# Pooled difference in its running sum's place, pooling output split from PSUM, another order of weight splits and s4 products

## The chip, the cores and the metric

The kernel runs on one core of a Trainium2 chip. The metric is the device time of one execution in microseconds (us), lower is better; it is given as the median of several executions. The engines are TensorE (PE, matrix products), VectorE (DVE), ScalarE (ACT) and GpSimd (POOL); SyncE (SP) only issues transfers. Each runs its own instructions in order and waits on semaphores for the others.

## The reference

One layer of an encoder block on 1024 tokens of width 1024, in float32. One projection gives q, k, v (eight attention heads of 64) and u (512 channels for pooling). Attention looks at a window of 8 x 16 on a token grid of width 64. The pooling takes a centred mean over 2, 4, 8 or 16 tokens, one window size for each group of 128 channels, subtracts the token and maps the difference with a 128 x 128 matrix and a scale per channel:

```
def multiscale_pool(u, w_pool, pool_scale):
    ...
        mean = (cg[:, hi] - cg[:, lo]) / (hi - lo).astype(jnp.float32)[:, None]
        outs.append(mean - uf[:, :, sl])
    d = jnp.stack(outs, axis=2).astype(u.dtype)
    y = jnp.einsum('btgc,gcd->btgd', d, w_pool).reshape(B, T, C)
    return y * pool_scale
...
        a = neighbourhood_attention(q, k, v, rpb[l])
        p = multiscale_pool(u, w_pool[l], pool_scale[l])
        x = x + jnp.concatenate([a, p], axis=-1) @ w_out[l]
        h2 = rms_norm(x, norm2_g[l])
        x = x + (jax.nn.silu(h2 @ w_gate[l]) * (h2 @ w_up[l])) @ w_down[l]
```

## The kernel before, in words

Float32 precision is had from three products: `split` (L118) writes a rounded high part `h` of an operand on ScalarE (L119) and the rest `l` = operand - `h` on VectorE (L120), and `mm3` (L132) multiplies high by high, high by low and low by high into the same PSUM bank. All matmuls have line L85, all transposes on TensorE L90, and all splits L119 and L120, so tiles are told apart by name, the high part of `dh`, `yh`, `w` or `bt_h` among them.

The stages in time: the first pass of projections (to about 40 us), the pooling stage (40 to 110), attention with the other projections between its steps (110 to 250), the output projection W_out with the last attention blocks between its steps (to 366), the gate and up products (366 to 791) and the down products (791 to 1001).

*Pooling.* `u_pool` runs over the four channel groups g. `u_mm(g)` multiplies out `u` of a group in two banks `pu`, which VectorE scales into `u` (L400). `u_win(g)` sums windows by doubling on VectorE (tiles `pw`, L418), corrects the edges (L422, L427), writes the difference `d` (L436), splits it into `dh` and `dl`, and multiplies by the group's matrix into two banks `py`. ScalarE scales these into `y` (L449) and with a permutation back to the order of the tokens; `y` is split once more, and GpSimd's queue stores both parts in `yd`. In the program `u_win(g - 1)` follows `u_mm(g)`; the order on VectorE, ScalarE and the queues is set by a scheduler, that on TensorE from L906 on by the program (`pin`). Weights of the next pass (`w1h`, `w1l` from `raw_w`) are split in between.

*Projections and attention.* `dense` is a generator of projection steps; each step is one run of 3 matmuls `pj` of 128x384. `run(R0)` takes 22 of them, then comes `u_win(3)`, then the space of the pooling's tiles is closed, and the attention's pool `ap` with the bias tiles `nb` is opened in it. `load_bias` (L590) loads two bias tiles on SP's queue, and GpSimd negates them (L591). Scores `s` get their bias on VectorE (L621), ScalarE takes the exponential (L631), GpSimd scales the result `e` (L639), TensorE transposes it (`pt`), it is split, and `po` = p times v follows. `vnh` and `vnl` are the two parts of v. The norm of q and k takes small steps on ScalarE and VectorE (`rsqrt`, L96 to L100) and a product (`qn`, L291), whose result TensorE transposes (`qkt`). `FIRST`, `CYC` and, for the last blocks, `WCYC` tell how many steps `more` takes from `dense` between two attention steps; in the W_out stage a step is 3 matmuls `pw`.

*Gate and up products.* They are formed in a Strassen-Winograd way: seven products of half blocks in place of eight, with weights `11`, `12`, `s1` to `s4`, `22` (`cook_w` splits one of them, L1060) and activations `11`, `21`, `t1` to `t4`, `22` (`split_op`). The first four products (EARLY) go together, part by part: `first` and `second` write bank `x`, `part_y` with `s2` and `t2` writes `y`, `part_z` and `part_w` write `z` and `w`, `part_4` adds `22` by `t4` to `z`, `part_5` adds `s4` by `22` to `w`. Each is 12 matmuls of 512 columns. `norm2` scales the normalized input (L1016), `sub` forms differences (L1030), `settle` ends an output (L1095 adds, L1100 and L1104).

Of the kernel before, what the change touches and what calls it, by code (L numbers as in the profile page):

```python
# [49 lines left out]
def hybrid_block(ctx, tc, xT, xt, w1, wu, rpbx, wpool, wout, wgu, wd, sm, out):  # L50
# [306 lines left out]
    def u_pool(up, hook):  # L357
# [46 lines left out]
        def u_win(g):  # L404
# [38 lines left out]
            for half in range(2):
                ps = bank((stp, pop)[half], f"py_{g}_{half}")
                hs = slice(half * 512, half * 512 + 512)
                mm3(ps, wph, wpl, dh[:, hs], dl[:, hs], True, True)
                pv = ps.rearrange("p (r k c e) -> p r k c e", r=2, k=4, c=8)
                for i in range(2):
                    nc.scalar.activation(  # L449
                        yv[:, 2 * half + i], pv[:, i], AF.Copy, scale=psc_sb[:, g : g + 1]  # L450
                    )
            ys = [slot(F32R, f"y{nm}_{g}") for nm in "hl"]
            split(*ys, y)
# [1154 lines left out]
```

## Time and profile before

| | us |
|---|---|
| median of 3 runs | 1006.23 (1005.81 to 1006.53) |
| the profiled execution | 1007.08 |
| its span | 1005.0 |
| TensorE busy | 989.8 (98%) |
| VectorE busy | 681.9 (68%) |
| ScalarE busy | 416.6 (41%) |
| GpSimd busy | 377.9 (38%) |
| mean granted clock of TensorE | 0.996 of full speed |

The profile is that of one execution; its rows give a start, a duration, the engine, the line, the operation, the tiles written and read and a count, and in brackets the idle time in front of the instruction and what ended it. Matmuls overlap: the duration of one is longer than the distance to the next, and the distance is what it costs. [...]

### The profile page before, as it was taken

To read this page: it belongs to the slowest core of one execution; us is meant where nothing else is said; L and a number is where in the kernel's file an instruction comes from. 1 tells how busy PE (TensorE), PEld (TensorE's weight loads), DVE (VectorE), ACT (ScalarE), POOL (GpSimd) and SP (SyncE) were. 2 spreads that over 40 slices of the span, in tenths; PEclk is the share of its full clock that TensorE was granted. 3 is DMA by queue.
4 is the path that set the end of the run, shared out by engine and by line. 5 is a ranking of instruction groups with operands and counts; after the bars stand their busy time and mean duration, and the time that the engine had idled before them with its cause. 6 is when DMAs were issued, how large, how long until landed. Compare 5 with 4: busy or idle time off the path is not lost.

```text
span 1005.0 us, 13257 instructions
## 1 busy us (share of the span) xinstructions
PE 989.8 (98%) x4801; PEld 843.2 (84%) x4801; DVE 681.9 (68%) x1087; ACT 416.6 (41%) x801; POOL 377.9 (38%) x423
## 2 busy tenths in 40 slices
PE   9997999999999999999999999999999999999998
PEld 9986999999788887878788888888888888888887
DVE  5677676656853789977975554555552599888872
ACT  6633566656643354434233233233242255442500
POOL 0100343323431510079866846846833400000170
PEclk9998999999999999999999999999999999999999
DMA  9411824135922420213423313313317983373302
GB/s 355 185 58 43 267 66 130 55 115 198 340 91 101 151 84 1 71 64 135 159 95 136 127 57 118 137 55 112 135 50 240 361 279 121 108 250 104 126 32 95
DMA packets 56322, 135.89 MB, mean 135 GB/s; under 512 B 5888, under 2 KB 14848, under 8 KB 56256
## 3 DMA queue, kind: packets, MB, share of 16 engines
q1 hardware_dynamic: 48176, 106.45, 31.5%
q0 software_dynamic: 6784, 24.38, 6.5%
q10 hardware_dynamic: 1296, 4.21, 1.1%
q8 instruction: 38, 0.62, 0.2%
q14 instruction: 28, 0.23, 0.1%
HBM read 98.05 MB, written 32.77 MB: 130 GB/s over the span
## 4 chain that ended last, share of the span: by engine, by line
PE 80%; DVE 10%; POOL 5%; issue 2%; ACT 2%; DMA 1%; DVEq 0%; POOLq 0%; ACTq 0%
PE pj L85 12%; PE w L85 9%; PE z L85 9%; PE x L85 8%; PE pw L85 6%; PE pc L85 6%; PE pa L85 6%; PE pd L85 6%; PE pu L85 4%; PE y L85 4%; PE pb L85 3%; PE po L85 3%; PE s L85 2%; PE pt L90 2%; POOL gr L1165 1%
## 5 line engine op out<-in xcount | busy, mean ns | idle before, releaser
L85 PE MATMUL x<-b_h,w 128*128 128x512 f32 x352 | 115.0, 389 | 0.0
L85 PE MATMUL pw<-mx,wo 128*128 128x512 f32 x384 | 90.4, 392 | 0.0
L85 PE MATMUL pj<-w1h,xh 128*128 128x384 f32 x256 | 88.0, 348 | 0.8 <-DVE vnl L306 0.6
L639 POOL TENSOR_SCALAR e<-e,r 64x128 f32<-64x128 f32 (+2 forms) x96 | 53.8, 575 | 90.2 <-DVE r L634 45.8
L85 PE MATMUL pj<-w1l,xh 128*128 128x384 f32 x256 | 85.2, 337 | 0.0
L85 PE MATMUL pj<-w1h,xl 128*128 128x384 f32 x256 | 84.5, 339 | 0.0
L85 PEld LDWEIGHTS pw<-mx,wo 128*128 128x128 f32 x384 | 71.1, 188 | 14.5 <-DVE mx L791 0.4
L1533 POOL TENSOR_TENSOR x2r<-x2r,u 128x512 f32<-128x512 f32 x12 | 23.8, 2015 | 149.8 <-issue 149.8
L1104 POOL TENSOR_TENSOR ur<-ur,gr 128x512 f32<-128x512 f32 x33 | 52.5, 1594 | 72.0 <-DVE ur L1095 49.3
L85 PEld LDWEIGHTS x<-b_h,w 128*128 128x128 f32 x352 | 66.1, 188 | 13.8 <-ACT ur L1109 0.2
L85 PE MATMUL x<-b_l,w 128*128 128x512 f32 x176 | 68.5, 389 | 0.0
L120 DVE TENSOR_TENSOR w_s<-sa,w_s 128x512 fp32r<-128x512 f32 x44 | 53.0, 1207 | 21.9 <-ACT w_s L119 21.5
L119 ACT CAST a_h<-raw_a 128x1024 fp32r<-128x1024 f32 (+1 forms) x42 | 41.0, 979 | 49.3 <-PE pc L85 13.8
L85 PE MATMUL w<-b_h,w_s 128*128 128x512 f32 x176 | 58.1, 391 | 0.6 <-DVE w_s L120 0.6
L85 PE MATMUL y<-bt_h,w_s 128*128 128x512 f32 x176 | 57.6, 390 | 0.8 <-ACT bt_h L119 0.8
L85 PE MATMUL z<-bt_h,w 128*128 128x512 f32 x176 | 57.9, 390 | 0.5 <-DVE gr L1095 0.5
L85 PE MATMUL w<-bt_h,w_s 128*128 128x512 f32 x176 | 57.8, 390 | 0.0
L85 PE MATMUL z<-bt_h,w_s 128*128 128x512 f32 x176 | 57.8, 389 | 0.0
L120 DVE TENSOR_TENSOR a_l<-raw_a,a_h 128x1024 fp32r<-128x1024 f32 (+1 forms) x42 | 49.9, 1193 | 3.4 <-ACT a_h L119 3.1
L85 PEld LDWEIGHTS pj<-w1h,xh 128*128 128x128 f32 x256 | 48.9, 192 | 2.3 <-DVE vnl L306 1.7
L85 PEld LDWEIGHTS pj<-w1h,xl 128*128 128x128 f32 x256 | 48.6, 191 | 0.0
L85 PEld LDWEIGHTS pj<-w1l,xh 128*128 128x128 f32 x256 | 48.5, 190 | 0.1
(275 smaller groups left out, 2639.9 us busy)
## 6 DMA issues: line engine op xcount, KB each, us to landing
raw_a<-gsd SPq DMA_DIRECT2D x77, 256.0 KB, 3.6
raw_g<-in_wgu SPq DMA_DIRECT2D x22, 512.0 KB, 3.9
raw_u<-in_wgu SPq DMA_DIRECT2D x22, 512.0 KB, 4.4
gsd<-gr POOLq DMA_DIRECT2D x22, 512.0 KB, 4.0
raw_d<-in_wd SPq DMA_DIRECT2D x20, 512.0 KB, 4.2
nb<-in_rpbx SPq DMA_DIRECT2D x24, 384.0 KB, 4.8
raw_w<-in_w SPq DMA_DIRECT2D x15, 384.0 KB, 5.3
gsd<-ur POOLq DMA_DIRECT2D x11, 512.0 KB, 3.2
```

The costliest lines, as they stand in the source:

```text
L85: i = nc.tensor.matmul(*a, **k)
L90: i = nc.tensor.transpose(*a)
L119: keep(nc.scalar.copy(h, src))
L120: keepd(nc.vector.tensor_tensor(out=l, in0=src, in1=h.bitcast(F32), op=ALU.subtract))
L639: nc.gpsimd.tensor_scalar(out=out, in0=in0, scalar1=s1, scalar2=1.0, op0=ALU.mult, op1=ALU.mult)
L1104: k(eng.tensor_tensor(out=res[i][c][:, l], in0=src, in1=g, op=ALU.mult))
L1165: tt = lambda **k: keepp(nc.gpsimd.tensor_tensor(**k))
L1533: nc.gpsimd.tensor_tensor(out=q, in0=q, in1=U2[c], op=ALU.add)
```

## The change

The window sums of a group now give way to the difference: `d` is written over the running sum (a view of `cur`), and the slot for `d` is gone. `dh` and `dl` are written in four pieces of 256 columns, permuted to the order of the tokens there, so that the bank `py` holds tokens in order. ScalarE then scales the bank into `yh` at once, and VectorE writes `yl` as the scaled bank minus `yh`, both from PSUM in pieces of 512 columns; the tile `y` and the last split are gone. `u_win(2)` leaves `u_pool` and stands behind the first four steps of `dense` (`R1`). `WCYC` takes one step more at two places. In the first chunk the weight `w_3_11` is loaded and split earlier, into a slot of its own, `w_3_12` and the low part for `s2` later, the second `t2` split stands ahead of an output step, and `part_4(1)` with its weight stands ahead of `part_5(0)`.

```
@@ -34,9 +34,10 @@
 WARM = 17
 CYC = [3, 3, 3, 4, 4, 4, 4, 4, 4, 4, 4, 5, 5, 5, 4, 4]
 R0 = 22
+R1 = 4
 FIRST = [3, 3, 4, 4, 4, 4, 4, 4, 4, 4, 4]
 CYC3 = CYC
-WCYC = [1, 4, 4, 1, 1] + [2] * 6 + [3]
+WCYC = [1, 5, 5, 1, 1] + [2] * 6 + [3]
 POOL_W = [2, 4, 8, 16]
 DGROUPS = [3, 4, 4]
 NPF = NFC // 2
@@ -430,27 +431,28 @@
                     in1=edge[:, g, 9 : 8 + hw],
                     op=ALU.mult,
                 )
-            d = slot(F32, f"d_{g}")
+            d = cur[:, o : o + T]
             dh = slot(F32R, f"dh_{g}")
             dl = slot(F32R, f"dl_{g}")
             nc.vector.scalar_tensor_tensor(
                 out=d, in0=cur[:, o : o + T], scalar=1.0 / w, in1=u[:, o : o + T], op0=ALU.mult, op1=ALU.subtract
             )
-            split(dh, dl, d)
-            y = slot(F32, f"y_{g}")
-            yv = y.rearrange("p (r c k e) -> p r k c e", r=4, c=8, k=4)
+            ys = [slot(F32R, f"y{nm}_{g}") for nm in "hl"]
+            dv = d.rearrange("p (r k c e) -> p r k c e", r=4, k=4, c=8)
+            hv, lv = (a.rearrange("p (r c k e) -> p r k c e", r=4, c=8, k=4) for a in (dh, dl))
+            for r in range(4):
+                split(hv[:, r], lv[:, r], dv[:, r])
             wph, wpl = wps[0][:, g], wps[1][:, g]
             for half in range(2):
                 ps = bank((stp, pop)[half], f"py_{g}_{half}")
                 hs = slice(half * 512, half * 512 + 512)
                 mm3(ps, wph, wpl, dh[:, hs], dl[:, hs], True, True)
-                pv = ps.rearrange("p (r k c e) -> p r k c e", r=2, k=4, c=8)
-                for i in range(2):
-                    nc.scalar.activation(
-                        yv[:, 2 * half + i], pv[:, i], AF.Copy, scale=psc_sb[:, g : g + 1]
-                    )
-            ys = [slot(F32R, f"y{nm}_{g}") for nm in "hl"]
-            split(*ys, y)
+                sc = psc_sb[:, g : g + 1]
+                yh, yl = (a[:, hs] for a in ys)
+                nc.scalar.activation(yh, ps, AF.Copy, scale=sc)
+                nc.vector.scalar_tensor_tensor(
+                    out=yl, in0=ps, scalar=sc, in1=yh.bitcast(F32), op0=ALU.mult, op1=ALU.subtract
+                )
             for nm in range(2):
                 nc.gpsimd.dma_start(out=yd[g][nm], in_=ys[nm].bitcast(F32))
 
@@ -464,9 +466,8 @@
             if g == 3:
                 cook_w1(1, 2)
                 cook_w1(1, 3)
-            if g:
+            if g in (1, 2):
                 u_win(g - 1)
-            if g in (1, 2):
                 cook_w1(1, g - 1)
         return u_win
 
@@ -904,7 +905,9 @@
 
     dense = g_dense()
     pin = True
-    run(R0)
+    run(R1)
+    u_win(2)
+    run(R0 - R1)
     u_win(3)
     su.close()
     sa = ExitStack()
@@ -1058,7 +1061,7 @@
         sums[i]["s1"], sums[i]["s2"] = s1, s2
 
     def cook_w(i, o):
-        if i < EARLY and o in ("11", "12"):
+        if i < EARLY and o in ("11", "12") and (i, o) != (3, "11"):
             w = rg.tile([P, 2, 512], F32R, tag="w", name=f"w_{i}_{o}")
         else:
             w = slot(F32R, f"w_{i}_{o}", [P, 2, 512])
@@ -1242,6 +1245,8 @@
     r6 = square1(6)
     hl.append(tok_split(r6, "s6"))
     w_full(7, 1)
+    fetch_w(3)
+    cook_w(3, "11")
     r7 = square1(7)
     hl.append(tok_split(r7, "s7"))
     cook_w(2, "11")
@@ -1255,11 +1260,8 @@
     tok_sum(1, hl[2], False, True)
     scale2(1, (lambda: sum_w(2, nc.vector, keepd),))
     first(1, xs[1], range(2, 4))
-    fetch_w(3)
     act_op("t2")
     norm2(1, 0, 2)
-    cook_w(3, "11")
-    cook_w(3, "12")
     second(0, xs[0])
     settle(0, 0, 0, xs[0])
     second(1, xs[1])
@@ -1269,14 +1271,15 @@
     norm2(1, 1, 3)
     first(2, xs[2])
     split_op("t2", 0, t2[0])
-    cook_w(0, "s2")
     first(3, xs[3])
+    cook_w(3, "12")
     second(2, xs[2])
     second(3, xs[3])
     sub(x2[1], x2[5], x2[1])
     sub(t2[1], x2[7], x2[1])
+    cook_w(0, "s2")
+    split_op("t2", 1, t2[1])
     settle(1, 0, 0, xs[1])
-    split_op("t2", 1, t2[1])
     cook_w(1, "s2")
     cook_w(2, "s2")
     settle(2, 0, 0, xs[2])
@@ -1318,18 +1321,18 @@
     cook_w(0, "22")
     part_w(2, mmp)
     part_z(3, mmp)
+    cook_w(1, "22")
     act_op("22")
     for q in range(2):
         split_op("22", q, x2[6 + q])
     cook_w(0, "s4")
     part_w(3, pop)
-    cook_w(1, "22")
     part_4(0)
+    part_4(1)
     cook_w(1, "s4")
     part_5(0)
     fetch_w(4)
     cook_w(2, "22")
-    part_4(1)
     cook_w(2, "s4")
     part_5(1)
     fetch_w(5)
```

On TensorE, at the end of the pooling's `u` products, stood before (`pu_1` is the second half of the last group, `py_0` and `py_1` the halves of group 2, `pj_0` the first projection bank; the last number of a name is a count of tiles):

```order
L85 MATMUL pu_1_948<-xl_212,wuh_820 128x512
L85 MATMUL pu_1_948<-xh_211,wul_821 128x512
L85 MATMUL py_0_998<-dh_992,wp_hl 128x512
L85 MATMUL py_1_1004<-dh_992,wp_hl 128x512
L85 MATMUL py_0_998<-dl_993,wp_hl 128x512
L85 MATMUL py_0_998<-dh_992,wp_hl 128x512
L85 MATMUL py_1_1004<-dl_993,wp_hl 128x512
L85 MATMUL py_1_1004<-dh_992,wp_hl 128x512
L85 MATMUL pj_0_1028<-w1h_0_814,xh_164 128x384
```

and stands now:

```order
L86 MATMUL pu_1_952<-xh_211,wul_823 128x512
L86 MATMUL pj_0_999<-w1h_0_816,xh_164 128x384
...
L86 MATMUL pj_1_1000<-w1h_0_816,xl_174 128x384
L86 MATMUL py_0_1034<-dh_1021,wp_hl 128x512
L86 MATMUL py_0_1034<-dl_1022,wp_hl 128x512
L86 MATMUL py_0_1034<-dh_1021,wp_hl 128x512
L86 MATMUL py_1_1040<-dh_1021,wp_hl 128x512
```

The six `py` of group 2 have moved behind twelve `pj`, and the two halves follow one another in place of alternating.

On VectorE, the rows from the edge corrections of group 2's window sum (`pw_4_987`, now `pw_4_1017`) to its low part `dl`; before:

```order
L422 TENSOR_TENSOR pw_4_987<-pw_4_987,edge 128x4
L427 TENSOR_TENSOR pw_4_987<-pw_4_987,edge 128x3
L400 TENSOR_TENSOR u_918<-pu_0_921,rstd_bc 128x8x4x8 x2
L120 TENSOR_TENSOR yl_907<-y_893,yh_906 128x1024
L120 TENSOR_TENSOR w1l_1_913<-raw_w_1_1_714,w1h_1_912 128x768
L120 TENSOR_TENSOR w1l_2_976<-raw_w_1_2_818,w1h_2_975 128x768
L400 TENSOR_TENSOR u_918<-pu_1_948,rstd_bc 128x8x4x8 x2
L418 TENSOR_TENSOR pw_1_1125<-u_918 128x1055
L120 TENSOR_TENSOR w1l_3_980<-raw_w_1_3_916,w1h_3_979 128x768
L436 SCALAR_TENSOR_TENSOR d_991<-pw_4_987,u_824 128x1024
L418 TENSOR_TENSOR pw_2_1127<-pw_1_1125 128x1052
L120 TENSOR_TENSOR dl_993<-d_991,dh_992 128x1024
```

and now:

```order
L453 SCALAR_TENSOR_TENSOR yl_893<-py_0_902,sm_sb,yh_892 128x512
L453 SCALAR_TENSOR_TENSOR yl_893<-py_1_908,sm_sb,yh_892 128x512
L423 TENSOR_TENSOR pw_4_1017<-pw_4_1017,edge 128x4
L428 TENSOR_TENSOR pw_4_1017<-pw_4_1017,edge 128x3
L121 TENSOR_TENSOR w1l_1_917<-raw_w_1_1_714,w1h_1_916 128x768
L121 TENSOR_TENSOR w1l_2_980<-raw_w_1_2_820,w1h_2_979 128x768
L437 SCALAR_TENSOR_TENSOR pw_4_1017<-pw_4_1017,u_826 128x1024
L401 TENSOR_TENSOR u_922<-pu_0_925,rstd_bc 128x8x4x8 x2
L121 TENSOR_TENSOR w1l_3_984<-raw_w_1_3_920,w1h_3_983 128x768
L121 TENSOR_TENSOR dl_1022<-pw_4_1017,dh_1021 128x4x8x8 x4
```

The difference (L436, now L437) stood behind both evacuations of `pu` and the first sum of group 3 (`pw_1_1125`), and now stands ahead of them.

On TensorE at the last attention block, around the transposes `pt_3` of the probabilities, to the first `po_3`; before:

```order
L90 MATMUL pt_3_1_3837<-ident,e_3_1_1_3707 128x128
L90 MATMUL pt_3_2_3838<-ident,e_3_1_1_3707 128x128
L85 MATMUL pw_0_0_3823<-mx_1_0_3132,wo_0_0_3086 128x512
L85 MATMUL pw_0_0_3823<-mx_1_1_3133,wo_0_0_3086 128x512
L85 MATMUL pw_0_0_3823<-mx_1_0_3132,wo_0_1_3087 128x512
L85 MATMUL pw_0_0_3823<-mx_1_0_3132,wo_0_0_3086 128x512
L85 MATMUL pw_0_0_3823<-mx_1_1_3133,wo_0_0_3086 128x512
L85 MATMUL pw_0_0_3823<-mx_1_0_3132,wo_0_1_3087 128x512
L85 MATMUL po_3_3861<-pt_h,vnh_2380 128x2x128
```

and now:

```order
L86 MATMUL pw_0_0_3831<-mx_1_0_3140,wo_0_1_3095 128x512
L91 MATMUL pt_3_0_3850<-ident,e_3_0_0_3704 128x128 x3
...
L91 MATMUL pt_3_1_3851<-ident,e_3_0_1_3708 128x128 x3
L91 MATMUL pt_3_1_3851<-ident,e_3_1_1_3721 128x128
L91 MATMUL pt_3_2_3852<-ident,e_3_1_1_3721 128x128
L86 MATMUL po_3_3869<-pt_h,vnh_2388 128x2x128
```

The six `pw` that stood between the last `pt` and `po` have moved ahead; the same count has moved ahead of the last `qkt`.

## Rows read from the trace of the kernel before

**Rows 1.** The page's busy line of all engines: us, share of the span, instructions.

```profile
PE 989.8 (98%) x4801; PEld 843.2 (84%) x4801; DVE 681.9 (68%) x1087; ACT 416.6 (41%) x801; POOL 377.9 (38%) x423
```

**Rows 2.** The view of TensorE's waits: who waited for whom, us in total, times, the longest.

```profile
PE py L85 <- ACT dh L119: 5.3, 1, 5.3
PE qkt L90 <- DVE qn L291: 1.2, 1, 1.2
...
PE y L85 <- ACT bt_h L119: 0.8, 1, 0.8
PE y L85 <- DVE bt_l L120: 0.8, 1, 0.8
...
PE w L85 <- DVE w_s L120: 0.6, 1, 0.6
```

**Rows 3.** The timeline of TensorE from 87 to 110 us: start, duration, line, operation, out<-in, shapes, count, and in brackets the idle time in front and its releaser.

```profile
87.77 0.39 PE L85 MATMUL pu<-xl,wuh 128*128 128x512 f32 x1
87.99 0.39 PE L85 MATMUL pu<-xh,wul 128*128 128x512 f32 x1
93.67 1.22 PE L85 MATMUL py<-dh,wp_hl 128*128 128x512 f32 x2 [5.29 <-ACT dh L119]
...
97.21 0.52 PE L85 MATMUL pj<-w1l,xh 128*128 128x384 f32 x1
97.53 0.52 PE L85 MATMUL pj<-w1h,xl 128*128 128x384 f32 x1
...
100.15 0.33 PE L85 MATMUL pj<-w1l,xh 128*128 128x384 f32 x1
100.32 0.33 PE L85 MATMUL pj<-w1h,xl 128*128 128x384 f32 x1
...
109.33 0.39 PE L85 MATMUL py<-dh,wp_hl 128*128 128x512 f32 x1
```

**Rows 4.** The windows of 2 us of TensorE: the window, its length, busy time and count, the granted clock, the share of the transfer engines and GB/s.

```profile
90.00:92.00 2.00, 0.00 (x0) 1.00 0.00 0
...
94.00:96.00 2.00, 1.88 (x4) 0.50 0.00 0
...
98.00:100.00 2.00, 2.00 (x11) 0.74 0.00 0
```

**Rows 5.** The timeline of VectorE from 79 to 93 us.

```profile
79.62 1.25 DVE L418 TENSOR_TENSOR pw<-pw 128x1048 f32<-128x1048 f32 x1
...
82.98 0.76 DVE L400 TENSOR_TENSOR u<-pu,rstd_bc 128x256 f32<-128x256 f32 x2 [1.84 <-PE pu L85]
84.08 1.23 DVE L120 TENSOR_TENSOR yl<-y,yh 128x1024 fp32r<-128x1024 f32 x1 [0.34 <-ACT yh L119]
85.22 1.82 DVE L120 TENSOR_TENSOR w1l<-raw_w,w1h 128x768 fp32r<-128x768 f32 x2
88.42 0.76 DVE L400 TENSOR_TENSOR u<-pu,rstd_bc 128x256 f32<-128x256 f32 x2 [1.38 <-PE pu L85]
...
90.45 0.95 DVE L120 TENSOR_TENSOR w1l<-raw_w,w1h 128x768 fp32r<-128x768 f32 x1
91.32 1.22 DVE L436 SCALAR_TENSOR_TENSOR d<-pw,u 128x1024 f32<-128x1024 f32 x1
```

**Rows 6.** What pieces of each size take: ScalarE's cast of 1024 columns and its four activations of 256 (timeline); VectorE's subtraction of 256 columns (the view of groups by form, 60 to 125 us: count, busy us, mean ns) and its three-operand form of 512 (timeline).

```profile
92.57 1.04 ACT L119 CAST dh<-d 128x1024 fp32r<-128x1024 f32 x1 [6.32 <-DVE d L436]
110.23 1.57 ACT L449 ACTIVATE y<-py,sm_sb 128x256 f32<-128x256 f32 x4 [1.67 <-PE py L85]
```

```profile
L120 DVE TENSOR_TENSOR kl<-qkt,kh 128x256 fp32r<-128x256 f32 x2 | 0.8, 418 | 0.4 <-ACT kh L119 0.4
```

```profile
378.04 2.08 DVE L1016 SCALAR_TENSOR_TENSOR x<-x,sm_sb,y 128x512 f32<-128x512 f32 x3
```

**Rows 7.** The first bias tiles: their load on SP's queue, GpSimd's negation and VectorE's first use (timelines), and the line on landing times of all bias loads from the view of the tile `nb`.

```profile
101.60 1.04 SPq L590 DMA_DIRECT2D nb<-in_rpbx  x2
107.13 1.64 POOL L591 TENSOR_SCALAR nb<-nb 128x768 f32<-128x768 f32 x2 [6.00 <-DVE v L260]
111.76 0.56 DVE L621 CUSTOM_DVE_ANT_0 e<-s,nb 128x384 f32<-128x384 f32 x1 [1.78 <-PE s L85]
```

```profile
DMA to landing us min/median/max: 3.1/4.8/9.0
```

**Rows 8.** The last attention block in the W_out stage: VectorE's and GpSimd's rows at 256 us, then the transposes, the splits of their result and the first product on TensorE, ScalarE and VectorE at 315 to 318 us (timelines).

```profile
256.84 2.40 DVE L99 SCALAR_TENSOR_TENSOR rsq_q<-rsq_q,v 128x8 f32<-128x8 f32 x1
256.81 1.62 POOL L639 TENSOR_SCALAR e<-e,r 64x128 f32<-64x128 f32 x4
...
315.15 1.25 PE L90 MATMUL pt<-ident,e 128*128 128x128 f32 x10
315.78 1.41 ACT L119 CAST pt_h<-pt 128x512 fp32r<-128x512 f32 x3 [3.78 <-PE pt L90]
316.40 1.62 DVE L120 TENSOR_TENSOR pt_l<-pt,pt_h 128x512 fp32r<-128x512 f32 x3 [8.81 <-ACT pt_h L119]
317.63 0.28 PE L85 MATMUL po<-pt_h,vnh 128*128 128x256 f32 x1
```

**Rows 9.** The timeline of VectorE in the first chunk: a row behind an idle stretch, the pair of low parts of `w_3`, and the low part of the first s4 weight.

```profile
371.15 0.69 DVE L120 TENSOR_TENSOR sq_hl_s<-sq,sq_hl_s 128x512 fp32r<-128x512 f32 x1 [1.35 <-ACT sq_hl_s L119]
...
380.69 1.29 DVE L120 TENSOR_TENSOR w<-raw_u,w 128x512 fp32r<-128x512 f32 x2
...
428.09 0.68 DVE L120 TENSOR_TENSOR w_s<-raw_g,w_s 128x512 fp32r<-128x512 f32 x1
```

More of the change, by code (lines that the diff above doesn't have):

```diff
@@ L36 @@
 R0 = 22
+R1 = 4
 FIRST = [3, 3, 4, 4, 4, 4, 4, 4, 4, 4, 4]
 CYC3 = CYC
-WCYC = [1, 4, 4, 1, 1] + [2] * 6 + [3]
+WCYC = [1, 5, 5, 1, 1] + [2] * 6 + [3]
 POOL_W = [2, 4, 8, 16]
@@ L432, in u_win @@
                 )
-            d = slot(F32, f"d_{g}")
+            d = cur[:, o : o + T]
             dh = slot(F32R, f"dh_{g}")
@@ L438, in u_win @@
             )
-            split(dh, dl, d)
-            y = slot(F32, f"y_{g}")
-            yv = y.rearrange("p (r c k e) -> p r k c e", r=4, c=8, k=4)
+            ys = [slot(F32R, f"y{nm}_{g}") for nm in "hl"]
+            dv = d.rearrange("p (r k c e) -> p r k c e", r=4, k=4, c=8)
+            hv, lv = (a.rearrange("p (r c k e) -> p r k c e", r=4, c=8, k=4) for a in (dh, dl))
+            for r in range(4):
+                split(hv[:, r], lv[:, r], dv[:, r])
             wph, wpl = wps[0][:, g], wps[1][:, g]
@@ L446, in u_win @@
                 mm3(ps, wph, wpl, dh[:, hs], dl[:, hs], True, True)
[L447 to L453, printed above, removed]
+                sc = psc_sb[:, g : g + 1]
+                yh, yl = (a[:, hs] for a in ys)
+                nc.scalar.activation(yh, ps, AF.Copy, scale=sc)
+                nc.vector.scalar_tensor_tensor(
+                    out=yl, in0=ps, scalar=sc, in1=yh.bitcast(F32), op0=ALU.mult, op1=ALU.subtract
+                )
             for nm in range(2):
@@ L466, in u_pool @@
                 cook_w1(1, 3)
-            if g:
+            if g in (1, 2):
                 u_win(g - 1)
-            if g in (1, 2):
                 cook_w1(1, g - 1)
@@ L906, in hybrid_block @@
     pin = True
-    run(R0)
+    run(R1)
+    u_win(2)
+    run(R0 - R1)
     u_win(3)
@@ L1060, in cook_w @@
     def cook_w(i, o):
-        if i < EARLY and o in ("11", "12"):
+        if i < EARLY and o in ("11", "12") and (i, o) != (3, "11"):
             w = rg.tile([P, 2, 512], F32R, tag="w", name=f"w_{i}_{o}")
@@ L1244, in hybrid_block @@
     w_full(7, 1)
+    fetch_w(3)
+    cook_w(3, "11")
     r7 = square1(7)
@@ L1271, in hybrid_block @@
     split_op("t2", 0, t2[0])
-    cook_w(0, "s2")
     first(3, xs[3])
+    cook_w(3, "12")
     second(2, xs[2])
@@ L1277, in hybrid_block @@
     sub(t2[1], x2[7], x2[1])
+    cook_w(0, "s2")
+    split_op("t2", 1, t2[1])
     settle(1, 0, 0, xs[1])
-    split_op("t2", 1, t2[1])
     cook_w(1, "s2")
@@ L1320, in hybrid_block @@
     part_z(3, mmp)
+    cook_w(1, "22")
     act_op("22")
@@ L1325, in hybrid_block @@
     part_w(3, pop)
-    cook_w(1, "22")
     part_4(0)
+    part_4(1)
     cook_w(1, "s4")
@@ L1331, in hybrid_block @@
     cook_w(2, "22")
-    part_4(1)
     cook_w(2, "s4")
```

3 lines of the change are left out of this document (removed).

## The prediction

> **What bounds the kernel now.** I read the page's busy line first: TensorE is busy 98% of the span [rows 1], so an edit can win only what TensorE idles, or what it does at a lower clock. The view of TensorE's waits then lists nearly all of that idle time in a handful of single events [rows 2]; one of 5.3 us stands out, the rest are about 1 us or less each. The timeline of TensorE places the large one: the last `pu` matmul starts at 87.99, the next instruction, `py` of pooling group 2, only at 93.67, released by the high cast of `d` on ScalarE [rows 3]. The windows show what follows: the granted clock was 1.00 until the idle stretch, 0.50 in 94 to 96 and 0.74 in 98 to 100 [rows 4], which is the lower level (1.2 GHz) for about 5 us. The matmuls say the same: 128x384 ones start 0.32 us apart at 97.21 and 97.53, 0.17 apart at 100.15 and 100.32 [rows 3].
>
> What that place costs in all: at full clock a 512-wide matmul takes 0.227 us of TensorE (87.77 to 87.99) and a 384-wide one 0.174. Between the end of `pu` (87.99 + 0.23 = 88.22) and `py` of group 3 stand 6 `py` and 66 `pj`: 6 x 0.227 + 66 x 0.174 = 12.85 us. `py` of group 3 could start at 101.07 and starts at 109.33 [rows 3]: 8.2 us lost, of which 5.3 are idle and 2.9 the lower clock.
>
> Why `d` was late stands in VectorE's rows [rows 5]. The windows of group 2 are summed by 80.87 (79.62 + 1.25). Then VectorE's own order puts the evacuation of `pu` of group 3 first, which waits 1.84 us for TensorE, `yl`, two weight splits, the second evacuation (another 1.38 us of waiting), the first sum of group 3 and a third weight split, and only then `d` at 91.32. VectorE was waiting for TensorE, and TensorE then for VectorE.
>
> **The change, part by part.**
>
> *Group 2 moved (R1 = 4).* Twelve `pj` matmuls now stand between the last `pu` and `py` of group 2, so TensorE asks for `dh` at 88.22 + 12 x 0.174 = 90.3. On VectorE `d` now stands ahead of the evacuations of `pu`: after 80.87 come the two new low parts of group 1 (2 x 0.69, the 128x512 form of [rows 6]), the edges (0.2), two weight splits (1.82, [rows 5]), then `d` (1.22): done at about 85.5. `dh` is now four ScalarE pieces of 128x256; the nearest row is four activations of that size, 1.57 us together, against 1.04 for the one 1024-wide cast that they replace [rows 6]: done at 87.1. `dl` is four VectorE pieces of 0.42 [rows 6] = 1.67 where one of 1.22 stood, behind one evacuation (0.76) and one weight split (0.95): done at about 88.9. Both are ready 1.4 us or more before TensorE asks. So the idle stretch goes, and with it the low clock, which only followed it: **-8.2 us**; bounds -8.2 and, if the pieces come 1.5 to 2 us later than I sum them, about -6. The evacuations of `pu` that now wait behind `d` (by some 2.5 us) hold no bank that TensorE needs before about 92.4, the fourth group of `pj`.
>
> [...]
>
> *Output of the pooling split from PSUM.* Per group ScalarE loses four activations (1.57) and a 1024-wide cast (1.04) and gains two 128x512 activations (about 0.6 each, a bound from 0.5 to 0.7 by the 128x256 and 1024-wide rows); VectorE loses a 1.22 us subtraction and gains two of 0.69. With the pieces of `dh` and `dl` added, ScalarE is 0.9 us a group lighter and VectorE 0.6 heavier. Neither bounds this stage once `d` is early; I cost it at nothing. The cover is the 54 `pj` between the two groups; without it the 0.6 would lie open.
>
> *`d` in place of the running sum.* The bias tiles `nb` take the space of the pooling's tiles, so their load has to wait for the last reader. Before, that was the write of `d` of group 3, and the load was issued at 101.60, to land 3.1 to 9.0 us later (median 4.8); GpSimd negated the two tiles from 107.13, and the scores' first VectorE step came at 111.76 [rows 7]. Now the last reader is the last piece of `dl` of group 3, and the load can go out at about 100.7, only 0.9 earlier, while TensorE is 8.2 us earlier. With the median landing the tiles are negated by 107.2, VectorE has the first scores done by about 109, then comes `vnl` of the next projection (0.35), which TensorE's `pj` needs by about 109.5. **+0.4 us**, bounds 0 and +1.2; beyond that it is a rival, below.
>
> *W_out steps (WCYC).* Six `pw` matmuls (6 x 0.227 = 1.36 us) go ahead of the last block's transposes `qkt`. There TensorE waited 1.2 us for `qn` [rows 2], whose chain held a 128x8 operation that took 2.40 us from 256.84 while GpSimd scaled `e` [rows 8]. The six cover that: -1.2, bounds 0 and -1.2. They are taken from between the last `pt` and `po`. There `pt` starts at 315.15 and ends its issue near 316.2, ScalarE casts from 315.78, VectorE subtracts from 316.40 (three, 1.62), and `po` began at 317.63, after the six [rows 8]. Without them TensorE reaches `po` at 316.2 and can't end it before the low parts come, around 317.5: **+1.3**, bounds +0.8 and +1.5. Together +0.1.
>
> *First chunk.* The high product's weight `w_3_11` (one VectorE piece, half of the 1.29 us pair at 380.69) goes into an idle 1.35 us at 371.15 [rows 9], `w_3_12` and `w_0_s2` go back behind the `t2` split. The TensorE waits at `y` for `bt_h` and `bt_l` are 0.8 each [rows 2]; the second half of that input comes about 1.2 us sooner, yet VectorE is busy all through, and the low part of `w_0_s2` then is the next to be late. I take **-0.6**, bounds 0 and -1.6. `fetch_w(3)` goes ahead on SP's queue with its DMAs and delays nothing that TensorE waits for.
>
> *Order of s4.* The wait of 0.6 at `w` is for the low part of the s4 weight, made at 428.09 [rows 2, 9]. Twelve matmuls of `part_4(1)` (12 x 0.227 = 2.7 us) now stand before it, and that weight is delayed only by one more split (0.68). **-0.6**, bounds -0.6 and 0.
>
> Sum: -8.2 + 0.4 + 0.1 - 0.6 - 0.6 = -8.9. The profiled execution took 1007.08 us, so 998.2; it lay 0.85 above the median of the runs (1006.23), so **997.4**.
>
> **The rivals.**
>
> *Late bias tiles (about 1000).* If `nb` lands at 7 rather than 4.8 us, `vnl` comes at about 111.5 and `pj` waits 2 us; again at the next block for 0.5: -8.9 + 2.5 = -6.4, 999.8. For it speaks that SP's load moved by 0.9 us and TensorE by 8.2; against, that the load has the queue for itself [rows 7]. It comes out the same by a second mechanism: GpSimd's two negations (1.64 us, [rows 7]) now fall beside VectorE's small rsqrt steps, and one such step took 2.40 us beside GpSimd's work at 256.84 [rows 8]; 1.6 us more before `vnl`, 999.6. [...]
>
> *The small orders give nothing (about 999.5).* W_out wins nothing at `qkt`, since what GpSimd and VectorE do there merely shifts, and loses 1.3 at `po`; the first chunk stays bound by VectorE: -8.2 + 0.4 + 1.3 - 0.6 = -7.1, 999.1. For it speaks VectorE's unbroken work there; against, that the six matmuls are there whatever VectorE does.
>
> *The gap moves on (about 1001).* `d` comes early, but the pieces of `dl`, written through a permuted view, take twice the 0.42 us, or `dl` waits for a slot that the store of group 1's `y` still reads: `py` of group 2 waits some 2 us, and the clock may fall for a part: -8.9 + 2 + 2 = -4.9, 1001.3.
>
> *Slower (about 1008).* The in-place `d` ties the first bias load to `dl` of group 3. If the load lands 11 us or more after its issue, VectorE's in-order queue holds `vnl` behind the scores' first step until about 115.5, `pj` stands still for 6 us from 109.5, and the clock drops as it did after 88 (another 2.9): the whole gain is given back, and a second block with the same 2 us late makes it 1008. It decides from 11 us on; the longest landing in the trace is 9.0 [rows 7], so it is unlikely.
>
> **How the numbers follow.** Forecast 997.4 (995.5 to 998.5): 0.55. Late bias tiles: 0.18. Small orders nothing: 0.12. The gap moves on: 0.07. Slower: 0.04; and 0.04 for no change that can be told. A measurement of this kernel can tell about 0.2% (2 us) from no change, so faster means below 1004.2. The low end of the range takes the favourable bounds of the small terms (-8.2 - 1.2 + 0.8 - 1.6 - 0.6 = -10.8: 995.4), the high end takes in the first two rivals and most of the third: 995.2 to 1001.5. Faster 0.91, same 0.05, slower 0.04.
>
> **What would show each step.** In the profile after: no wait of `py` on ScalarE and a granted clock of 1.00 from 88 to 100; `py` of group 3 near 101 (right: -8.2). A new wait of `pj` on `vnl` near 109 to 112 of under 1 us (if 2 or more, the first rival). No wait at the last `qkt`; a wait of `po` on `pt_h` or `pt_l` of about 1.3 near 306 (if none, the W_out term is a gain). The waits of `y` on `bt_h` and `bt_l` cut by half, none of `w` on `w_s` after `part_4`. The prediction is wrong if `py` of group 2 still waits or if the clock falls elsewhere in the first 130 us.

## The result and the profile after

The changed kernel takes 997.95 us (median of 4 runs, 997.62 to 998.92) against 1006.38 (1005.81 to 1006.72) for the kernel before beside it: 0.9918 of its time, 95% interval 0.9901 to 0.9936. On another chip, beside the last experiments, it took 999.78 (998.31 to 1000.74) against 1006.10: 0.9933, interval 0.9919 to 0.9947. Two executions of the experiments, one of the first run with 5673 us and one of the seventh with 1228 us, lie far outside all others and stand in no median, range or view below. The profiled execution took 997.62 us with a span of 995.5, 9.5 less than before. The forecast was 997.4, in a range of 995.2 to 1001.5, with 0.55 on 995.5 to 998.5; the median of the second chip lies outside the narrower one.

TensorE's waits after, the view that answers to [rows 2]:

```profile
PE z L86 <- DVE gr L1098: 1.1, 1, 1.1
PE pj L86 <- DVE vnl L307: 0.7, 1, 0.7
PE po L86 <- ACT pt_h L120: 0.6, 1, 0.6
PE w L86 <- DVE bt_l L121: 0.5, 1, 0.5
PE po L86 <- DVE pt_l L121: 0.4, 1, 0.4
PE y L86 <- DVE bt_l L121: 0.3, 1, 0.3
```

The 5.3 us of `py` are gone, as are the waits of `qkt`, of `y` for `bt_h` and of `w` for `w_s`. New are the two of `po` and the one of `w` for `bt_l`, and `z` waits 1.1 where it waited 0.5.

The timeline of TensorE and the windows of its granted clock, as a share of full speed, where [rows 3, 4] had the gap:

```profile
87.91 0.39 PE L86 MATMUL pu<-xh,wul 128*128 128x512 f32 x1
...
90.24 0.39 PE L86 MATMUL py<-dh,wp_hl 128*128 128x512 f32 x1
...
100.99 0.39 PE L86 MATMUL py<-dh,wp_hl 128*128 128x512 f32 x1
```

```profile
90.00:92.00 2.00, 2.00 (x12) 1.00 0.00 0
...
94.00:96.00 2.00, 2.00 (x14) 1.00 0.66 266
```

No idle time, clock 1.00, and `py` of group 3 at 100.99 in place of 109.33. The timelines of VectorE and of ScalarE show why, against [rows 5]: after the low parts of group 1 (80.70 to 82.10) and two weight splits comes `d` (written into `pw`, L437), and only then an evacuation of `pu` (L401).

```profile
82.17 1.82 DVE L121 TENSOR_TENSOR w1l<-raw_w,w1h 128x768 fp32r<-128x768 f32 x2
83.91 1.22 DVE L437 SCALAR_TENSOR_TENSOR pw<-pw,u 128x1024 f32<-128x1024 f32 x1
85.04 0.74 DVE L401 TENSOR_TENSOR u<-pu,rstd_bc 128x256 f32<-128x256 f32 x2
...
86.57 1.42 DVE L121 TENSOR_TENSOR dl<-pw,dh 128x256 fp32r<-128x256 f32 x4
```

```profile
85.21 1.33 ACT L120 CAST dh<-pw 128x256 fp32r<-128x256 f32 x4 [2.61 <-DVE pw L437]
```

`d` ends at 85.13, the four pieces of `dh` at 86.54, those of `dl` at 87.99. The bias tiles, against [rows 7] (timelines of SP's queue, GpSimd and VectorE, and the one wait of `pj` on TensorE):

```profile
99.97 0.80 SPq L591 DMA_DIRECT2D nb<-in_rpbx  x2
103.39 0.83 POOL L592 TENSOR_SCALAR nb<-nb 128x768 f32<-128x768 f32 x1 [8.08 <-DVE yl L453]
104.26 0.56 DVE L622 CUSTOM_DVE_ANT_0 e<-s,nb 128x384 f32<-128x384 f32 x1 [0.21 <-POOL mixf L68]
...
123.15 0.45 PE L86 MATMUL pj<-w1h,xh 128*128 128x384 f32 x1 [0.67 <-DVE vnl L307]
```

The load goes out at 99.97, only 1.6 us earlier than before, but GpSimd can start on the first tile 3.4 us later; TensorE doesn't wait near 109. It waits at 122.5 for `vnl`, 0.67 us, where it waited 0.64 before, 8 us later.

The view of waits doesn't show all that TensorE loses. Its lead, by which a matmul starts earlier than the same one of the kernel before, is 8.34 us at `py` of group 3 and 7.92 at the scores of the next block (120.01 before, 112.09 now). The 0.42 between them are lost in the first scores, which go in pairs; the rows of one pair before and now:

```profile
111.45 0.33 PE L85 MATMUL s<-kh,qh 64*128 64x384 f32 x2
```

```profile
103.11 0.75 PE L86 MATMUL s<-kh,qh 64*128 64x384 f32 x2
```

The second of the pair starts at 103.42, 0.31 behind the first. The first of VectorE's two new `yl` pieces (two from 102.61 on, 1.44 us) had by then just read its bank `py`; that the scores wait for it is named as the releaser only in the profile of the kernel with `d` in its own slot, below.

### The profile page after: what moved, and what is told of

It reads as the page before. It is cut to its first block, busy times and chain, and to the rows that moved or that the text cites. A ratio compares the mean times of both kernels' runs of the same rounds, so it can differ in the third digit from the quotient of the medians.

```text
span 995.5 us, 13274 instructions
## 1 busy us (share of the span) xinstructions
PE 986.9 (99%) x4801; PEld 841.5 (85%) x4801; DVE 685.0 (69%) x1103; ACT 412.4 (41%) x801; POOL 376.0 (38%) x423
## 4 chain that ended last, share of the span: by engine, by line
PE 50%; DVE 0%; issue 0%
PE z L86 9%; PE w L86 8%; PE x L86 8%; PE pc L86 6%; PE pa L86 6%; PE pd L86 6%; PE y L86 4%; PE pb L86 3%; PE pd_end L86 0%; DVE gr L1098 0%; DVE w L121 0%; DVE x2r L1494 0%
```

## The experiments

**The move undone (first and fifth run).** `u_win(2)` goes back to its place, all else stays:

```
-            if g in (1, 2):
+            if g:
                 u_win(g - 1)
+            if g in (1, 2):
                 cook_w1(1, g - 1)
...
-    run(R1)
-    u_win(2)
-    run(R0 - R1)
+    run(R0)
```

> The changed kernel with u_win(2) back in u_pool, so that py of group 2 follows the last pu at once again; the new splits, the in-place d and everything else stay. Theory A (d was late by its place in VectorE's order, and the rewritten u_win alone brings it ahead of the evacuations of pu): VectorE's order is that of the changed kernel, dh is ready near 86.5 and dl near 88.0, TensorE asks at 88.1: idle under 0.5 us, granted clock 1.00, 998 us within 1.5. Theory B (the twelve pj matmuls are the cover): the idle time of about 5 us before py comes back with the low clock, 1004 to 1006 us.

> The kernel of the first experiment once more, since the execution that was profiled there ran five times too long throughout. Theory A (VectorE's order): before py of group 2 under 0.5 us of idle time, d done at about 85.1 and dl at 88.0, granted clock 1.00, 998 to 1001 us. Theory B (the twelve pj): about 5 us idle, low clock, 1004 to 1006.

Measured: 998.85, 999.49 and 1001.12 in the first, 0.9935 of the kernel before (0.9918 to 0.9952); 999.82 (997.40 to 1000.59) in the second, 0.9940 (0.9927 to 0.9953). The timeline of TensorE in the second:

```profile
87.87 0.39 PE L86 MATMUL pu<-xh,wul 128*128 128x512 f32 x1
88.10 0.62 PE L86 MATMUL py<-dh,wp_hl 128*128 128x512 f32 x2
...
100.92 0.39 PE L86 MATMUL py<-dh,wp_hl 128*128 128x512 f32 x1
```

`py` of group 2 follows the last `pu` without a gap, and `py` of group 3 starts at 100.92, as in the changed kernel. Theory A: the twelve `pj` are not what closes the gap, as long as `d` is written in place (more below).

**The move alone.** The kernel before, and nothing but:

```
+R1 = 4
...
-            if g:
+            if g in (1, 2):
                 u_win(g - 1)
-            if g in (1, 2):
                 cook_w1(1, g - 1)
...
-    run(R0)
+    run(R1)
+    u_win(2)
+    run(R0 - R1)
```

> The kernel before with R1 = 4 alone (u_win(2) behind twelve pj); splits, d, y, WCYC and first chunk as before. VectorE's order keeps d behind both evacuations of pu. Theory A: dh still comes at about 93.6, TensorE asks at 90.3 and waits about 3.3 us; the twelve pj (2.1 us) are all that is won if the clock falls as before, 1004 us, or 1001 if it stays at 1.00. Theory B: the move alone brings the whole gain of this place, 998 to 999 us.

Measured: 1004.31 (1003.34 to 1005.18), 0.9983 (0.9974 to 0.9992). VectorE's `d` and TensorE's `py` of group 2 (timelines):

```profile
90.73 1.22 DVE L437 SCALAR_TENSOR_TENSOR d<-pw,u 128x1024 f32<-128x1024 f32 x1
```

```profile
93.14 0.50 PE L86 MATMUL py<-dh,wp_hl 128*128 128x512 f32 x1 [3.24 <-ACT dh L120]
94.43 0.79 PE L86 MATMUL py<-dl,wp_hl 128*128 128x512 f32 x1 [0.80 <-DVE dl L121]
...
106.50 0.39 PE L86 MATMUL py<-dh,wp_hl 128*128 128x512 f32 x1
```

`d` still starts at 90.7, TensorE waits 3.2 and 0.8 us, the clock falls again (0.54 in 94 to 96), and `py` of group 3 comes only 2.8 us earlier, 0.6 of which this execution was ahead before the place (its last `pu` starts at 87.40 against 87.99). Both runs together: the gain comes from the rewritten `u_win`, under which the scheduler puts `d` ahead of the evacuations. The move adds 2 us of cover that this order doesn't need. Which part of the rewriting brings the order about (the pieces, the output from PSUM, `d` in place) was tested for the last alone.

**The idle time filled.** The kernel before, with work that nobody reads in the gap:

```
+            if g == 2:
+                fill = bank(stp, "fill")
+                for _ in range(22):
+                    mm(fill, wph, xh[KC - 1][:, 512:1024], start=True, stop=True)
```

> The kernel before with 22 added matmuls of 512 columns into an unused bank between the last pu and py of group 2; their result is not read. They take 22 x 0.227 = 5.0 of the 5.3 us of idle time, so that only the clock differs. Theory (the 2.9 us behind the idle stretch are the lower clock, and it falls because TensorE stood still): py starts at about 93.7 as before, the granted clock stays 1.00, py of group 3 starts near 106.5 and the time is 2.9 us lower, 1003.5. Rival (the low clock has another cause): 1006.4, clock 0.5 in 94 to 98 as before.

Measured: 1005.26 (1003.21 to 1005.57), 0.9983 (0.9973 to 0.9994). TensorE's timeline, and its windows further on:

```profile
88.22 5.15 PE L85 MATMUL fill<-xh,wp_hl 128*128 128x512 f32 x22
93.68 0.73 PE L85 MATMUL py<-dh,wp_hl 128*128 128x512 f32 x2 [0.31 <-ACT dh L119]
95.03 0.51 PE L85 MATMUL py<-dl,wp_hl 128*128 128x512 f32 x1 [0.61 <-DVE dl L120]
...
107.51 0.39 PE L85 MATMUL py<-dh,wp_hl 128*128 128x512 f32 x1
...
390.23 0.50 PE L85 MATMUL y<-bt_h,w_s 128*128 128x512 f32 x1 [0.79 <-ACT bt_h L119]
391.49 0.50 PE L85 MATMUL y<-bt_l,w_s 128*128 128x512 f32 x1 [0.76 <-DVE bt_l L120]
```

```profile
392.00:394.00 2.00, 2.00 (x7) 0.65 0.00 0
394.00:396.00 2.00, 2.00 (x6) 0.50 0.00 0
```

The clock stays at 1.00 from 84 to 118, so it was the idle time that let it fall. But `py` of group 3 comes only 1.8 us earlier (107.51 against 109.33), not 2.9. `py` starts at the same time as before (93.68 against 93.67; the 0.31 for `dh` are what the filling left of the old gap), and the first `py` with `dl` too (95.03 against 95.02): `dl` is late by itself. At full clock the two `py` ahead of it take 2 x 0.227 of these 1.35 us, so 0.9 us are lost to `dl` even at full clock. The median is only 0.9 us lower: behind the two waits of `y` in the first chunk the clock fell in this profile (0.65, 0.50), which it did not in that of the kernel before (1.00 in both windows, waits of 0.84 and 0.76).

**Later bias tiles.** In `load_bias` of the changed kernel:

```
+            for _ in range(3 if p == b == 0 else 1):
                 keeps(nc.sync.dma_start(out=nb, in_=rpbx[p, COLPAT[b], :, H]))
```

> The changed kernel with the first two bias tiles loaded three times over, each load behind the one before, so that they come about 7 us later (near 110.5 in place of 103.4). First rival's mechanism (the bias tiles are close to the critical path): VectorE's scores wait until about 111.5, TensorE reaches the scores of the next block at 112.1 and waits 1 to 3 us for their banks, 999 to 1001 us; if VectorE's queue also holds vnl, 2 us more. Rival (a late load costs nothing here): 998 us within 0.7.

Measured: 1003.32 (1002.32 to 1004.83), 0.9970 (0.9959 to 0.9982). VectorE's first scores, and the longest of TensorE's waits for them (timelines):

```profile
112.52 0.56 DVE L623 CUSTOM_DVE_ANT_0 e<-s,nb 128x384 f32<-128x384 f32 x1 [4.85 <-POOL nb L593]
```

```profile
115.77 0.92 PE L86 MATMUL s<-kh,qh 64*128 64x384 f32 x2 [1.36 <-DVE m L623]
```

The scores come 8.3 us later, and the kernel takes about 4 us more than the changed one (0.9970 against 0.9918 and 0.9933), more than either theory said: besides waits of 0.5 and 1.4 us for the scores and 1.3 for `vnl` the clock is 0.66 in 115 to 120. The added loads also push back all that stands behind them on SP's queue (the first `vsh` goes out at 109.62 in place of 100.88), so the 4 us aren't the price of the bias tiles alone. GpSimd has the first tile 11.2 us after the load's issue, the delay from which the prediction's rival *Slower* has the whole gain given back: about half of it was. The step that this rival needed, `vnl` held behind the scores, did not come: VectorE has one `vnl` at 106.69, ahead of the scores at 112.52. So late bias tiles cost; in the changed kernel they were not late.

**Old first chunk, old s4, old WCYC.** Three kernels, each the changed one with one order set back. The first, the weights of the first chunk:

```
-        if i < EARLY and o in ("11", "12") and (i, o) != (3, "11"):
+        if i < EARLY and o in ("11", "12"):
...
-    fetch_w(3)
-    cook_w(3, "11")
     r7 = square1(7)
...
+    fetch_w(3)
     act_op("t2")
     norm2(1, 0, 2)
+    cook_w(3, "11")
+    cook_w(3, "12")
...
+    cook_w(0, "s2")
     first(3, xs[3])
-    cook_w(3, "12")
...
-    cook_w(0, "s2")
-    split_op("t2", 1, t2[1])
     settle(1, 0, 0, xs[1])
+    split_op("t2", 1, t2[1])
```

> The changed kernel with the old order of the first chunk's weights (w_3_11, w_3_12, w_0_s2 and the second t2 split; the order of s4 stays new). Theory: the two waits of 0.8 us at y come back in place of 0.32 and 0.45, +0.8 us: 998.8. The clock fell behind that pair of waits in the profiles of two experiments so far, though not in that of the kernel before; where it does, 2 us more, 1000.8, so that the single times lie in two groups. Rival (VectorE is behind by as much either way): 998.0 and no second group.

Measured: 1000.20 (998.76 to 1002.16), 0.9955 (0.9942 to 0.9968). TensorE's two waits come back:

```profile
384.28 0.49 PE L86 MATMUL y<-bt_h,w_s 128*128 128x512 f32 x1 [0.79 <-ACT bt_h L120]
...
385.54 0.50 PE L86 MATMUL y<-bt_l,w_s 128*128 128x512 f32 x1 [0.77 <-DVE bt_l L121]
```

They are 0.79 and 0.77. In the changed kernel one of 0.32 is left there, and the 0.45 stand elsewhere, at `w` (397.21), where this kernel has none. By TensorE's lead the first chunk wins 0.60 in the changed kernel (8.11 ahead of it, 8.71 behind) and 0.03 here (8.01, 8.04): 0.6 is what the order is worth in the profiles. The times can't show it: the median is 1.0 to 1.5 above those of the two kernels below, in times that spread over 3.4. The clock stayed at 1.00 behind the waits in this profile; two of the five executions had a mean clock of 0.998, which is no proof of the place.

The second, the order of s4:

```
-    cook_w(1, "22")
     act_op("22")
...
+    cook_w(1, "22")
     part_4(0)
-    part_4(1)
...
     cook_w(2, "22")
+    part_4(1)
```

> The changed kernel with part_4(1) and the 22 weight of 1 back behind part_5(0). Theory: the wait of 0.6 us of w for the low part of the s4 weight comes back, 998.5. The wait of 1.1 us of z for gr near 490 stays if GpSimd's row of products sets it, or falls to 0.5 if this order made it: 997.9. Rival: the whole of it is given back further on, 998.0 and no wait at w.

Measured: 998.66 (998.13 to 1001.90), 0.9940 (0.9928 to 0.9952), and no profile that tells of waits. Inconclusive; that the wait of `w` goes is seen in the profile after alone, and whether the new order made the longer wait of `z` stays open.

The third, the table of W_out:

```
-WCYC = [1, 5, 5, 1, 1] + [2] * 6 + [3]
+WCYC = [1, 4, 4, 1, 1] + [2] * 6 + [3]
```

> The changed kernel with the old WCYC. Theory (a swap of one wait for another): the wait of 1.2 us of qkt for qn comes back, the two waits of po (0.6 and 0.4) go, 998.2. Rival (the change at qkt is pure gain): 999.1, with the waits of po unchanged. Rival (the change costs): 997.0, with no wait at qkt.

Measured: 999.16 (996.24 to 1000.97), 0.9938 (0.9926 to 0.9951). From the view of TensorE's waits:

```profile
PE pj L86 <- DVE vnl L307: 2.0, 1, 2.0
...
PE qkt L91 <- DVE qn L292: 1.2, 1, 1.2
```

The wait of `qkt` is back, no `po` waits: a swap, as the theory had it. By TensorE's lead from the first `pw` to the last, W_out wins 0.27 in the changed kernel (7.84 to 8.11) and 0.02 here (6.34 to 6.36). Such a difference can't be seen in times that spread over 4 us.

**What spreads them: the changed kernel again, and with fewer loads.** The second is the changed kernel with two lines in `load_bias`:

```
+            if p == 0 and b == 1:
+                nbs[p, 1, H] = nbs[p, 0, H]
+                continue
```

> The changed kernel itself, as the measure for the three kernels beside it on the same chip: 0.992 of the kernel before. Its wait of pj for vnl near 122 us is 0.7 us in its first profile and 1.6 to 2.0 in those of the last experiments, in a stretch in which weight and bias loads land one behind the other; if that is a matter of when they land and not of the edits, it lies in the same range here.

> The changed kernel without the bias load of the second block (it uses the first block's bias tiles, so the bias of that block is another one), 768 KB less between 107 and 122 us. Theory (since TensorE is 8 us earlier there, the loads are what is late at 122): the wait of pj for vnl near 122 falls under 0.4 us, 0.5 to 1.5 us less than the changed kernel, single times closer together. Rival (that wait comes from VectorE's and GpSimd's own work): 0.7 to 2.0 as before, same time.

Measured: 999.78 (998.31 to 1000.74) and 996.92 (996.63 to 997.55), 0.9933 (0.9919 to 0.9947) and 0.9909 (0.9895 to 0.9922). Of the first: TensorE's wait, two windows of its clock, and what ScalarE and GpSimd waited for ahead of it; then TensorE's wait in the second:

```profile
123.35 0.45 PE L86 MATMUL pj<-w1h,xh 128*128 128x384 f32 x1 [1.75 <-DVE vnl L307]
```

```profile
124.00:126.00 2.00, 2.00 (x12) 0.56 0.00 0
126.00:128.00 2.00, 2.00 (x13) 0.58 0.00 0
```

```profile
115.34 0.83 ACT L120 CAST w1h<-raw_w 128x768 fp32r<-128x768 f32 x1 [3.97 <-DMA raw_w<-in_w]
```

```profile
116.38 2.28 POOL L592 TENSOR_SCALAR nb<-nb 128x768 f32<-128x768 f32 x2 [2.45 <-DMA nb<-in_rpbx]
```

```profile
122.11 0.45 PE L86 MATMUL pj<-w1h,xh 128*128 128x384 f32 x1 [0.53 <-DVE vnl L307]
```

With 768 KB less the wait is 0.53 in place of 1.75 (under 0.4 was forecast), the clock stays up, and the times lie within 0.9 us of each other. The edit also takes two negations off GpSimd, so by itself it doesn't tell the loads from GpSimd's work. The rows of the first do: ScalarE stands still until a weight load lands, with its exponentials behind that cast (from 116.08), and GpSimd until bias tiles land, with its scaling of `e` behind them (118.64; 116.87 in the second). So the landing of the loads is the cause of the larger wait.

In the first, TensorE's lead falls from 8.79 to 6.18 us over this stretch, 2.6 in all with about 1.5 of it the clock; in the first profile of the same kernel it falls by 0.1. Of the 2.5 between them 0.9 give back a head start: this execution was already 0.9 further ahead at its last `pu` (87.02 against 87.91), while the loads landed at about the same time. Among its five executions the three with a mean granted clock of 0.998 took 999.78 to 1000.74, the two at 1.00 took 998.31 and 998.53; that this is the clock behind 122 us is seen for the profiled one alone.

**`d` in its own slot.** The changed kernel with

```
-            d = cur[:, o : o + T]
+            d = slot(F32, f"d_{g}")
```

> The changed kernel with d in a slot of its own again; splits, y and the move stay. VectorE's order has d of group 2 behind the first evacuation of pu, and dl in two halves around the second. Theory (in place or not matters little): the bias load goes out some 2.7 us earlier (near 97.3 in place of 100), py of group 2 waits up to 0.7 us, time within 0.8 us of the changed kernel. Rival (the in-place d ties down the loads, and they are the new limit): 1 to 2 us faster.

Measured: 998.21 (997.60 to 999.33), 0.9921 (0.9909 to 0.9934). VectorE's `d` and the second half of `dl`, and TensorE's scores (timelines):

```profile
85.61 1.22 DVE L437 SCALAR_TENSOR_TENSOR d<-pw,u 128x1024 f32<-128x1024 f32 x1
...
91.02 0.75 DVE L121 TENSOR_TENSOR dl<-d,dh 128x256 fp32r<-128x256 f32 x2
```

```profile
104.76 0.44 PE L86 MATMUL s<-kh,qh 64*128 64x384 f32 x1 [0.55 <-DVE yl L453]
```

`d` stands behind the first evacuation of `pu` here (84.08) and `dl` in two halves behind the second (88.51), so the last low parts come at 91.77, and `py`, behind the twelve `pj`, still waits 0.3. In place or not does matter to the order: with `d` in its own slot the move would be needed, by these times (`pu` ends at 88.2); it was not run without it. The bias load goes out 7.7 us behind `py` of group 2 (98.16 against 90.42), in the changed kernel 9.7; the scores wait 0.55 for the `yl` that reads the bank `py`, and no `pj` waits for `vnl` at all. The median is 1.6 us under that of the changed kernel beside it, but the intervals overlap; the rival is favoured, not shown.

**Two repairs.** The changed kernel with

```
-WCYC = [1, 5, 5, 1, 1] + [2] * 6 + [3]
+WCYC = [1, 5, 5, 1, 1] + [2, 2, 1, 2, 2, 1] + [3]
...
-            sum_w(i + 2)
+            if i + 2 == 8:
+                sum_w(8, nc.vector, keepd)
+            else:
+                sum_w(i + 2)
```

The second edit aims at these rows of the changed kernel, VectorE's and GpSimd's timelines near 480 us (the first and the last of GpSimd's six rows):

```profile
480.17 8.16 DVE L121 TENSOR_TENSOR w_s<-sa,w_s 128x512 fp32r<-128x512 f32 x1
```

```profile
480.27 1.30 POOL L1058 TENSOR_TENSOR sa<-raw_g,raw_g 128x512 f32<-128x512 f32 x1
...
486.48 1.28 POOL L1168 TENSOR_TENSOR gr<-ur 128x512 f32<-128x512 f32 x1
```

> The changed kernel with two repairs. WCYC ends so that the six pw stand before the last po again, taken three each from two earlier places: the waits of po (0.6 and 0.4) go, that of qkt stays away. The sums of the weights of chunk 8 go from GpSimd to VectorE, which takes three of the six products in a row that GpSimd ran beside a subtraction of VectorE of 8.16 us near 480: the wait of z for gr (1.1) falls to 0.5 or less. Theory: 1.5 to 2 us less than the changed kernel. Rival for the second (VectorE's three added sums make gr as late): 1.0 less, and z still waits 1.

Measured: 996.32 (995.96 to 997.29), 0.9903 (0.9890 to 0.9917), the fastest of the kernels that compute the whole layer. The waits of `po` and of `z` are gone from TensorE's view, that of `qkt` stays away, and the same subtraction of VectorE takes:

```profile
484.01 1.78 DVE L121 TENSOR_TENSOR w_s<-sa,w_s 128x512 fp32r<-128x512 f32 x1
```

The median is 3.5 us under the changed kernel's, with 1.5 to 2 forecast. The waits of `po` and `z` are 2.1 of it; the rest would be the wait at 122 us, 1.34 in this profile, and the clock behind it, which stayed at 1.00 here. Neither edit touches that place, so this part is the loads' doing and not the repair's; it is read from one profile of each.

## Why the prediction was right

- **The sum.** -8.9 was forecast for the profiled execution, -9.5 came (1007.08 to 997.62); between the medians it was -8.4. By TensorE's lead: 8.34 at `py` of group 3; 0.50 lost until the first `pw`; 0.27 won in W_out, 0.60 in the first chunk, 0.85 around s4; 0.32 lost where `z` waits; 0.22 won behind the last matmul. Some of the closeness is luck: group 2 came for another reason than its heading says, the +0.4 of the bias tiles came from another place, and `z` was not forecast.
- **Group 2, -8.2.** The size held, and so did the times on the way: `d` at 85.1 (85.5 forecast), `dh` 86.5 (87.1), `dl` 88.0 (88.9), TensorE at 90.2 (90.3). The pieces cost 0.33 and 0.36 us each, not 0.39 and 0.42. The heading was wrong: the step was put down to the move. What the text says of VectorE, that `d` now stands ahead of the evacuations, is the whole of it, and the rewritten `u_win` brings that about, `d` in place among it. The move alone brings 1.9 us of median, the rewrite without the move nearly all.
- **Its lower clock, 2.9 of the 8.2.** That it only follows the idle time is shown by the filled gap, where it stayed at 1.00 from 84 to 118. Its 1.2 GHz are, by [rows 3], a rate: at the clock of 0.50 matmuls of 384 columns start 0.32 us apart, 1.2 columns a ns, and at 1.00 0.174 us, 2.2. The size is wrong: the clock was worth 1.8 (109.33 to 107.51), and 0.9 were `dl`, which came late at either clock. The -8.2 stands, since the new order brings `dl` early too.
- **The output from PSUM, costed at nothing.** It cost 0.42 us, as the starts and the one named releaser have it. `yl` now reads the bank `py`, in VectorE's order behind `qn`, and the scores that follow group 3 wait for the bank (0.55 us where the wait is named, with `d` in its own slot). The prediction asked whether the engines were full, and not when the bank comes free.
- **The pieces of `dh` and `dl`.** Four small ones cost more here than one large one, but less than forecast: ScalarE's four take 1.33 us (1.57 forecast, 1.04 for one cast), VectorE's four 1.42 (1.67 forecast, 1.22 for one subtraction). The 1.57 is a row of pieces read from PSUM; those of `dh` are read from SBUF.
- **Bias tiles, +0.4.** At the place named nothing waits; GpSimd began on the first tile 3.4 us after the load's issue, and the forecast had 4.8. The small rsqrt steps of VectorE took 0.17 us each from 101.27, before GpSimd's negations at 103.39, so the second mechanism of that rival had nothing to collide with (its sum is off too: 1.6 more than 997.4 is 999.0, not 999.6). With `d` in its own slot the negations start at 101.50 and one such step, at 102.58, takes 0.68. The mechanism behind the term is real one block later, for weight and bias loads together: 0.7 to 2.0 us at 122 us, where the kernel before waited 0.64, and the clock with it in some executions. In the changed kernel's profile on the second chip it took 2.6 us of TensorE's lead, about the first rival's price.
- **W_out, +0.1.** The swap that was forecast, a little better: -1.2 and +1.0 by the waits, -0.27 by the lead.
- **First chunk, -0.6.** -0.60 by the lead, though not as told: the wait of `y` for `bt_h` goes altogether, that for `bt_l` falls from 0.76 to 0.32, and a new one of 0.45 comes at `w`.
- **s4, -0.6.** The wait of 0.58 goes and the lead grows by 0.85 there. No run separates it.
- **Not forecast: `z`.** Its wait grows from 0.5 to 1.1. The prediction followed no transfer of work past 440 us. GpSimd's products came back to back beside a subtraction of VectorE (8.16 us, against 1.78 with the two repairs), and `gr`, for which `z` waits, stood behind that subtraction in VectorE's order. The two repairs show that this is the wait. What brought the products together, the new order of s4 or the earlier TensorE, stays open, so a part of the gain of s4 may be given back here.

## What to carry to other kernels

When an engine idles for a result of another, look at what stands ahead of that result in the other's in-order queue, and whether that itself waits for the first engine; if the order in that queue can be changed, work put into the gap is not needed (without the move `py` of group 3 started at 100.92, with it at 100.99). Price an idle stretch of TensorE with the slow clock behind it (1.8 us behind 5.3 here), but ask which operands would have been late at full clock as well (`dl`, 0.9 us). Where an engine takes over the reading of a PSUM bank, ask when it frees the bank (0.42 us here). Compare the starts of the same instruction in both kernels: that loss, where the two matmuls of a pair start 0.31 us apart, stood in no view of waits of the changed kernel. Behind the 8.3 us gained here the loads of the next stage were the next thing to be late, by 0.67 us in one profile of the changed kernel and 1.75 in another: look at them in several executions, since one profile shows one execution.
